# First stage of a hybrid diffusion block: modulation weights first, turning product with the row factor, projections in step, and decay rows laid out contiguously

## The chip, the cores and the metric

One core of a Trainium2 chip runs the whole program. The metric is device microseconds of one execution, lower is better. The engines are TensorE (PE, with its weight loads PEld), VectorE (DVE), ScalarE (ACT), GpSimd (POOL) and SyncE (SP), which issues nearly all DMAs. Each engine works through its own instructions in order; SP's DMAs go out in order on one queue that 16 DMA engines serve.

## The reference, cut to what matters

One layer of a diffusion backbone for 1024 tokens and 256 context tokens of width 1024. Each token row is normalised and modulated, projected by `w_in`, mixed by three branches (S5, Mamba-2, RG-LRU), merged by gates, and passed to a mixture of experts.

```python
def _rmsnorm(x, g):
    y = x32 * lax.rsqrt(jnp.mean(x32 * x32, axis=-1, keepdims=True) + EPS)
    return (y * g).astype(x.dtype)
def _modulate(x, g, shift, scale):          # shift, scale: columns of silu(c) @ w_mod + b_mod
    return _rmsnorm(x, g) * (1 + scale) + shift
proj = h @ p['w_in']                        # u_s5, z, xbc, dt_raw, x_lru, g_lru, gates
# Mamba-2, per chunk of 128 tokens, direction and head:
lmat = jnp.exp(_segsum(a))                  # exp of differences of cumulated decays, masked
y_diag = einsum(cb * lmat, xs);  y_off = einsum(cm, entering) * exp(a_cum)
```

## The kernel before, in words

All matrix products with large weights are made of two parts: the weight and the activation are split into a rounded part (`hi`, type fp32r) and a rest (`lo`), and `mm3` (L265 to L267) multiplies hi·hi, hi·lo and lo·hi.

**First stage (L154 to L254).** SP issues in this order: the eight 128x1024 row tiles of x (`xts`, half a MB each) with small parameters between them, the raw weights of two `u` projections, eight 1 MB pieces `wm` of the modulation weight, two context tiles, the `dt` weight. `x_norm` squares a row tile on ACT, gets the row factor by DVE and POOL, and scales the tile on DVE. PE turns it in 128x128 blocks by transposes (`xtb`), and ACT and DVE copy the blocks into `xh0`. When `wm` has landed, PE multiplies it with silu(c) (`pm`), and the columns `gs` and `modT` are made. `modulate` (L222 to L225) then makes `hxh` on ACT, the full value on DVE and `hxl` on DVE or POOL, for two halves of 512 tokens and, from the turned context, `hch` and `hcl`. The `dt` projection multiplies unsplit values (`pdt`, fp32) in four column groups of 32. The planner (a simulated timeline at build time) orders the instructions of each engine by priority and readiness.

**Second stage, `p1` (L290 to L657).** Tables of S5 powers (`lam`, `arai`, `pw`, `den`, `cB`), then the projections `u`, `xb`, `xl`, `gl` by `proj_chunk`, and the S5 scans by `s5_tab` and `s5_dat`.

**Third stage, `p2` (L683 to L945).** The states of Mamba-2 (`states`, tiles `xk`, `xd`, `st`), then 32 times `chunk(g, c)` (L785 to L831), with z and gate projections (`pj_z`, `pj_gt`), RG-LRU (`lps`, `lr`, `li`) and the rest of the modulation (`wm`, `pm`, L909, L912) between them. `chunk` loads a 512 KB tile `rowb`: for two directions and four heads the cumulated decays of 128 tokens, repeated on all 128 partitions. ACT makes `dec` of it (L796), eight DVE instructions subtract a column of `XL` and limit (L801), ACT takes the exponential (L802), POOL adds the directions (L803), DVE multiplies with `pcb` (L804), POOL scales `dec` (L805), and PE multiplies (`yps`, L814 and L815). The three buffers of `rowb` come round in turn. The row source `rowsd` is written once, [4 groups, 2 directions, 4 heads, 1024 tokens].

Of the kernel before, what the change touches and what calls it, by code (L numbers as in the profile page):

```python
# [18 lines left out]
P = 128  # L19
# [11 lines left out]
NEP = 4  # L31
NHI = 4
# [7 lines left out]
HXP = (1, 4, 7)  # L40
HXC = (0, 2, 4, 6)
# [4 lines left out]
LAG = 2  # L46
MEN = {mybir.EngineType.DVE, mybir.EngineType.Pool, mybir.EngineType.Activation, mybir.EngineType.PE}
# [17 lines left out]
def backbone(ctx: ExitStack, tc: tile.TileContext, I, out, dbg=None, stop=None):  # L65
# [19 lines left out]
    def bank(name):  # L85
        return bankh[0](name)
# [22 lines left out]
    dtb = cp.tile([P, 1], F32, name="dtb")  # L109
# [32 lines left out]
    pre = {}

    def x_load(i):
        Y.dma_start(xts[i], dap(I["x"] if i < 8 else I["ctx"], (i % 8) * P * D, [[D, P], [1, D]]))

    def x_norm(i):
        xt = xts[i]
        jk = p0x.tile([P, D], mybir.dt.bfloat16, tag="jk", name=f"jk{i}", bufs=1)
        A.activation(jk, xt, AF.Square, accum_out=ss[:, i:i + 1])  # L150
        v = p0x.tile([P, 2], F32, tag="v", name=f"v{i}", bufs=10)
        V.tensor_scalar(xt, xt, rstd_of(ss[:, i:i + 1], v), None, op0=ALU.mult)

    with tc.high_priority(offset=20000):  # L154
        with tc.tile_pool(name="p0", bufs=1, reuse_waits="tile") as p0:
            wms = [p0.tile([P, 2048], F32, name=f"wm{j}") for j in range(KC)]
# [10 lines left out]
            for i in range(8):  # L167
                x_load(i)
# [3 lines left out]
            for q in range(2):  # L172
                pre[f"u{q}"] = load_w(I["w_in"], 7200, OFF_U + q * P, P, KC, f"u{q}")
            for j in range(KC):
                Y.dma_start(wms[j], dap(I["w_mod"], j * 6 * D, [[KC * 6 * D, P], [1, 2048]]))
            for i in range(8, 10):
                x_load(i)
            Y.dma_start(wdt, dap(I["w_in"], OFF_DT, [[7200, P], [P * 7200, KC], [1, 32]]))
            for j in range(4):
                Y.dma_start(dtb[32 * j:32 * j + 32, :], dap(I["m2_dt_bias"], 0, [[1, 32], [1, 1]]))  # L180
            A.activation(scc, craw, AF.Silu)
            pm = bank("pm")
            V.memset(pm, 0.0)
            for i in range(8):
                x_norm(i)
                for h in range(2):
                    tb = bank(f"xtb{i}_{h}")
                    for q in range(4):
                        k = 4 * h + q
                        T.transpose(tb[:, q * P:(q + 1) * P], xts[i][:, k * P:(k + 1) * P], ident)  # L190
                    dst = xh0[:, 4 * h:4 * h + 4, i * P:(i + 1) * P]
                    (V.tensor_copy if h else A.copy)(dst, tb.rearrange("p (q c) -> p q c", q=4))
# [8 lines left out]
            mrow = p0x.tile([98, 512], F32, name="mrow")  # L201
# [20 lines left out]
        def modulate(k, e, src, t, hh, ll, E):  # L222
            A.activation(hh, src, AF.Identity, bias=modT[:, k, e:e + 1], scale=gs[:, k, e:e + 1])
            V.tensor_scalar(t, src, gs[:, k, e:e + 1], modT[:, k, e:e + 1], op0=ALU.mult, op1=ALU.add)
            E.tensor_sub(ll, t, hh.bitcast(F32))  # L225

        for h in range(2):
            sl = slice(h * 512, (h + 1) * 512)
            for k in range(KC):
                x_ = xh0[:, k, sl]  # L230
                modulate(k, 0, x_, x_, hxh[k][:, sl], hxl[k][:, sl], G if k in HXP else V)
        for i in range(8, 10):
            x_norm(i)
        for k in range(KC):
            tb = bank(f"xtc{k}")
            for i in range(2):
                T.transpose(tb[:, i * P:(i + 1) * P], xts[8 + i][:, k * P:(k + 1) * P], ident)
            modulate(k, 1, tb[:, 0:256], xc0[:, k, :], hch[k], hcl[k], G if k in HXC else V)

        pdt = psp.tile([P, 512], F32, tag="pm", name="pdt", bufs=1)  # L240
        for o, ng, n, src in ((0, 4, 256, xh0), (256, 2, P, xc0)):
            for k in range(KC):
                for j in range(ng):
                    T.matmul(pdt[32 * j:32 * j + 32, o:o + n], wdt[:, k, :], src[:, k, j * n:(j + 1) * n], start=(k == 0), stop=(k == KC - 1))
        dtT = xts[0]
        A.activation(dtT[:, 0:256], pdt[:, 0:256], AF.Identity, bias=dtb)
        A.activation(dtT[0:64, 256:384], pdt[0:64, 256:384], AF.Identity, bias=dtb[0:64])
        pd = bank("pd")
        dv = dt.rearrange("p (c e) -> p c e", c=10)
        for h in range(2):  # L250
            T.transpose(pd[:, h * P:(h + 1) * P], dtT[:, h * P:(h + 1) * P], ident)
            V.tensor_copy(dv[:, h:8:2], pd[:, h * P:(h + 1) * P].rearrange("p (j e) -> p j e", j=4))
        T.transpose(pd[:, 256:320], dtT[0:64, 256:384], ident[:64, :64])
        V.tensor_copy(dv[:, 8:10], pd[:, 256:320].rearrange("p (j e) -> p j e", j=2))  # L254
# [34 lines left out]
    with tc.tile_pool(name="p1", bufs=1, reuse_waits="tile") as p1:  # L289
        NT = 19  # L290
        lam = p1.tile([P, 2, 32], F32, name="lam")
        pl = bank("pl")
        for e, nm in enumerate(("s5_lam_re", "s5_lam_im")):
            ln = p1.tile([32, 2, 64], F32, tag="ln", name=f"ln{e}", bufs=2)
            Y.dma_start(ln, dap(I[nm], 0, [[64, 32], [2048, 2], [1, 64]]))
            T.transpose(pl[:, e * 32:(e + 1) * 32], ln.rearrange("g d p -> g (d p)"), ident[:32, :32])
        V.tensor_copy(lam, pl[:, 0:64].rearrange("p (e g) -> p e g", e=2))
        step = p1.tile([P, 32], F32, name="step")
        for d in range(2):
            Y.dma_start(step[64 * d:64 * d + 64, :], dap(I["s5_log_step"], 32 * d, [[0, 64], [1, 32]]))  # L300
# [355 lines left out]
    if dbg is not None:  # L656
        emit("s5", s5_dram)  # L657
# [903 lines left out]
```

## Time and profile before

| what | value |
|---|---|
| median of 3 runs | 2121.89 us (2120.39 to 2122.43) |
| the profiled execution | 2120.92 us, span 2119.1 us |
| PE busy in the span | 1919.3 us, 91% |
| DVE, ACT, POOL busy | 1525.2, 1020.3, 510.4 us |
| first stage ends on PE with the last `pj_u` product | 96.1 us |
| chunks of the third stage | 680 to 1040 us |
| mean granted clock of TensorE | 0.956 |

The span is the profiled part of the profiled execution; 1.8 us lie around it. A busy PE is one with a product in flight, not one at its peak, and its speed follows the granted clock: 1.00 is 2.4 GHz, 0.50 is 1.2 GHz.

### The profile page before, as it was taken

The page shows a single profiled execution, that of the slowest core. Times are in us where ns is not written, and L with a number is a line of the kernel's source. Part 1 is how long each engine was busy: PE and PEld are TensorE (multiplying, and loading weights), DVE is VectorE, ACT ScalarE, POOL GpSimd, SP SyncE. Part 2 cuts the span into 40 slices and gives each one's busy share as a digit, 9 for nine tenths or more (in the row PEclk, how much of TensorE's full clock was granted, in tenths as well). Part 3 has the DMA queues.
Part 4 walks back from the last instruction along what each step waited for, and adds up shares of the span by engine and source line. Part 5 has one row for each costly group of instructions (what it writes and reads, how often), then busy time and mean ns, then how long its engine had stood idle before and what let it go on. Part 6 is the DMA issues. An engine that isn't in the chain of part 4 may idle for free.

```text
span 2119.1 us, 27213 instructions
## 1 busy us (share of the span) xinstructions
PE 1919.3 (91%) x9630; PEld 1516.2 (72%) x9630; DVE 1525.2 (72%) x2232; ACT 1020.3 (48%) x1313; POOL 510.4 (24%) x489
## 2 busy tenths in 40 slices
PE   5989999988889988879999999898299999999997
PEld 2678888877657666456577888687188888888885
DVE  4787788783454777667434655628899999999998
ACT  4434434432213665446332212222188888888785
POOL 1353333330142344233100000234501111100122
PEclk9999999999999999989999999999599999999999
DMA  8234334422586676777666554554599999999983
GB/s 313 54 81 114 101 95 117 122 90 90 180 261 192 186 212 175 242 180 210 208 174 188 180 160 153 186 200 149 196 339 381 400 389 404 387 389 393 391 312 137
DMA packets 301554, 462.67 MB, mean 218 GB/s; under 512 B 39945, under 2 KB 200121, under 8 KB 300393
## 3 DMA queue, kind: packets, MB, share of 16 engines
q1 hardware_dynamic: 297096, 445.19, 62.2%
q0 software_dynamic: 4320, 15.73, 2.9%
q8 instruction: 76, 1.25, 0.2%
q14 instruction: 62, 0.50, 0.1%
HBM read 384.44 MB, written 78.51 MB: 218 GB/s over the span
## 4 chain that ended last, share of the span: by engine, by line
PE 55%; DMA 9%; DVE 7%; issue 2%; ACT 1%; SPq 1%; POOL 1%; DVEq 0%; ACTq 0%; POOLq 0%
PE h_w L1443 6%; PE h_w L1445 6%; PE h_w L1444 6%; PE wo L1268 3%; DMA rowb<-rowsd 3%; PE py_w L1445 3%; PE py_w L1443 3%; PE py_w L1444 3%; PE pj_gt L267 2%; PE pj_gt L265 2%; PE pj_gt L266 2%; DMA wm<-in_w_mod_dram 2%; PE bom L266 1%; PE bom L265 1%; PE st L752 1%
## 5 line engine op out<-in xcount | busy, mean ns | idle before, releaser
L1338 DVE TENSOR_TENSOR el_w<-er_w,eh_w 128x1024 fp32r<-128x1024 f32 x384 | 460.7, 1220 | 25.0 <-ACT eh_w L1337 11.1
L1337 ACT CAST eh_w<-er_w 128x1024 fp32r<-128x1024 f32 x384 | 403.7, 1052 | 135.4 <-PE h_w L1444 58.9
L1443 PE MATMUL h_w<-eh_w,thi_x 128*128 128x512 f32 x512 | 202.9, 396 | 0.0
L1445 PE MATMUL h_w<-el_w,thi_x 128*128 128x512 f32 x512 | 200.2, 391 | 0.0
L1444 PE MATMUL h_w<-eh_w,tlo_x 128*128 128x512 f32 x512 | 199.8, 390 | 0.0
L801 DVE SCALAR_TENSOR_TENSOR rowb<-rowb,XL,lim 128x128 f32<-128x128 f32 x256 | 116.1, 518 | 72.1 <-ACT dec L796 72.1
L265 PE MATMUL pj_gt<-hxh,whi_gt 128*128 128x512 f32 x384 | 155.9, 406 | 11.9 <-ACT gz L779 11.9
L267 PE MATMUL pj_gt<-hxh,wlo_gt 128*128 128x512 f32 x384 | 155.3, 404 | 0.0
L266 PE MATMUL pj_gt<-hxl,whi_gt 128*128 128x512 f32 x384 | 155.1, 404 | 0.0
L1445 PEld LDWEIGHTS h_w<-el_w,thi_x 128*128 128x128 f32 x512 | 96.2, 188 | 20.4
L1444 PEld LDWEIGHTS h_w<-eh_w,tlo_x 128*128 128x128 f32 x512 | 96.5, 188 | 19.6 <-DVE tlo_x L1362 0.4
L1443 PEld LDWEIGHTS h_w<-eh_w,thi_x 128*128 128x128 f32 x512 | 96.5, 188 | 19.2 <-ACT thi_x L1361 0.2
L265 PEld LDWEIGHTS pj_gt<-hxh,whi_gt 128*128 128x128 f32 x384 | 74.4, 194 | 38.0 <-ACT gz L779 16.1
L1346 POOL DMA_INDIRECT xs<-h2d,idx x16 | 23.3, 1459 | 309.5 <-PE tb_x L1354 294.4
L1443 PE MATMUL py_w<-eh_w,thi_h 128*128 128x512 f32 x240 | 96.3, 401 | 0.0
L1445 PE MATMUL py_w<-el_w,thi_h 128*128 128x512 f32 x240 | 94.0, 392 | 0.0
L1444 PE MATMUL py_w<-eh_w,tlo_h 128*128 128x512 f32 x240 | 93.5, 390 | 0.0
L267 PEld LDWEIGHTS pj_gt<-hxh,wlo_gt 128*128 128x128 f32 x384 | 74.4, 194 | 25.4 <-issue 9.6
L266 PEld LDWEIGHTS pj_gt<-hxl,whi_gt 128*128 128x128 f32 x384 | 74.4, 194 | 20.5 <-issue 4.9
L796 ACT ACTIVATE dec<-rowb 64x512 f32<-64x512 f32 x64 | 40.2, 629 | 82.7 <-DMA rowb<-rowsd 72.7
L267 PE MATMUL pj_xb<-hxh,wlo_xb 128*128 128x512 f32 x192 | 76.8, 400 | 0.5 <-DVE wlo_xb L128 0.5
L265 PE MATMUL pj_xb<-hxh,whi_xb 128*128 128x512 f32 x192 | 76.7, 399 | 0.0
(653 smaller groups left out, 4894.7 us busy)
## 6 DMA issues: line engine op xcount, KB each, us to landing
er_w<-in_moe_w_dram SPq DMA_DIRECT2D x384, 512.0 KB
wm<-in_w_mod_dram SPq DMA_DIRECT2D x32, 512.0 KB
rowb<-rowsd SPq DMA_DIRECT2D x32, 512.0 KB
raw_gt<-in_w_in_dram SPq DMA_DIRECT2D x24, 512.0 KB
gtd<-gz SPq DMA_DIRECT2D x48, 256.0 KB
xk<-xed SPq DMA_DIRECT2D x18, 512.0 KB
wm<-in_w_mod_dram SPq DMA_DIRECT2D x8, 1024.0 KB
xe<-xed SPq DMA_DIRECT2D x32, 256.0 KB
```

The source lines that it names most:

```text
L265: T.matmul(ps, wh(k), xh(k), start=(first and k == 0), stop=False)
L266: T.matmul(ps, wh(k), xl(k), start=False, stop=False)
L267: T.matmul(ps, wl(k), xh(k), start=False, stop=(last and k == nk - 1))
L796: A.activation(dec[64 * d:64 * d + 64], rowb[64 * d:64 * d + 64, d], AF.Exp)
L801: V.scalar_tensor_tensor(rowb[:, d, h], rowb[:, d, h], XL[:, c, d, 4 * g + h:4 * g + h + 1], lim[:, d], op0=ALU.subtract, op1=ALU.min)
L1268: T.matmul(st4[i]["ps"][n], ms[i][a][:, k], wo[k][b][:, sl], start=(k == 0 and q == 0), stop=(k == KC - 1 and q == 2))
L1337: A.copy(a, raw)
L1338: V.tensor_sub(b, raw, a.bitcast(F32))
L1346: G.indirect_dma_start(out=xsb[e], out_offset=None, in_=h2d[:, :], in_offset=bass.IndirectOffsetOnAxis(ap=idx[:, e:e + 1], axis=0))
L1443: T.matmul(ps[n], xa[:, j, :], a[:, sl], start=(j == 0), stop=False)
L1444: T.matmul(ps[n], xb[:, j, :], a[:, sl], start=False, stop=False)
L1445: T.matmul(ps[n], xa[:, j, :], b[:, sl], start=False, stop=(j == KC - 1))
```

## The change

The first stage gets its order for DVE, ACT and PE as it is written. SP first loads the small S5 inputs and c, then all of `wm`, then x0 to x3, the raw weights of `u`, x4 to x7; the context tiles are loaded into the slots of x2 and x3 once these have been turned. The S5 tables are made in this stage ahead of `pm`. x isn't scaled any more: a diagonal tile `dg` holds the row factors, and a full fp32 product of x with `dg` turns and scales at once. `modulate` reads that product from PSUM, uses no POOL, and the `u` products follow two steps behind it. The `dt` projection moves into `p1`, behind the `u` stores, and takes the split activations with a 64-column split weight. In `p2`, `rowsd` is laid out so that what one chunk needs lies in 4 KB without a gap; two whole-tile DVE instructions replace the eight, and the add goes from POOL to DVE.

```diff
+    def x_dg(i):
+        dgs[i] = p0x.tile([P, P], F32, tag="dg", name=f"dg{i}", bufs=8)
+        V.tensor_scalar(dgs[i], ident, rss0[i], None, op0=ALU.mult)
...
+    with tc.high_priority(offset=20000), tc.manual_schedule(engines=MEN3):
...
+            for j in range(KC):
+                Y.dma_start(wms[j], dap(I["w_mod"], j * 6 * D, [[KC * 6 * D, P], [1, 2048]]))
...
+            for i in range(8):
                 x_load(i)
+                for q in range(2 if i == 3 else 0):
+                    uraw.append(wp.tile([P, KC, P], F32, tag="raw", name=f"raw_u{q}", bufs=3))
+                    Y.dma_start(uraw[q], dap(I["w_in"], OFF_U + q * P, [[7200, P], [P * 7200, KC], [1, P]]))
...
+        def modulate(k, e, src, t, hh, ll):
+            sc, bi = gs[:, k, e:e + 1], modT[:, k, e:e + 1]
+            A.activation(hh, src, AF.Identity, bias=bi, scale=sc)
+            if k in HXA:
+                A.activation(t, src, AF.Identity, bias=bi, scale=sc)
+            else:
+                V.tensor_scalar(t, src, sc, bi, op0=ALU.mult, op1=ALU.add)
+            V.tensor_sub(ll, t, hh.bitcast(F32))
+        def turned(tiles, k):
+            tb = bank(f"xt{tiles[0]}k{k}")
+            for q, i in enumerate(tiles):
+                T.matmul(tb[:, q * P:(q + 1) * P], xts[i][:, k * P:(k + 1) * P], dgs[i], start=True, stop=True)
+            return tb[:, 0:len(tiles) * P]
...
+        for i in range(4):
+            x_sq(i)
+            if i > 0:
+                x_dg(i - 1)
+        u_cast(0)
+        x_dg(3)
+        for hf in range(3):
...
+                tb = turned(tiles, k)
...
+                if (hf, k) >= (0, 2):
+                    ready(*divmod(8 * hf + k - 2, 8))
+                    drain(1 if hf == 1 else 2)
...
+        for c in range(10):
+            T.matmul(pd[:, 32 * c:32 * c + 32], dtT[c // 4][0:64, (c % 4) * P:(c % 4 + 1) * P], twice, start=True, stop=True)
...
-            Y.dma_start(dap(rowsd, d * 4 * S, [[8 * S, 4], [S, 4], [1, S]]), rw[16 * d:16 * d + 16])
+            for g in range(4):
+                Y.dma_start(dap(rowsd, g * 8 * S + d * 512, [[P, 4], [8 * P, 8], [1, P]]), rw[16 * d + 4 * g:16 * d + 4 * g + 4].rearrange("h (c q) -> h c q", c=8))
...
-            Y.dma_start(rowb.rearrange("p d h q -> p (d h) q"), dap(rowsd, g * 8 * S + q0, [[0, P], [S, 8], [1, P]]))
+            Y.dma_start(rowb.rearrange("p d h q -> p (d h q)"), dap(rowsd, (8 * g + c) * 8 * P, [[0, P], [1, 8 * P]]))
...
-            for d in range(2):
-                for h in range(4):
-                    V.scalar_tensor_tensor(rowb[:, d, h], rowb[:, d, h], XL[:, c, d, 4 * g + h:4 * g + h + 1], lim[:, d], op0=ALU.subtract, op1=ALU.min)
+            sh = [P, 2, 4, P]
+            V.tensor_sub(rowb, rowb, XL[:, c, :, 4 * g:4 * g + 4][:, :, :, None].to_broadcast(sh))
+            V.tensor_tensor(rowb, rowb, lim[:, :, None, :].to_broadcast(sh), op=ALU.min)
             A.activation(rowb, rowb, AF.Exp)
-            G.tensor_add(rowb[:, 0], rowb[:, 0], rowb[:, 1])
+            V.tensor_add(rowb[:, 0], rowb[:, 0], rowb[:, 1])
```

## Rows read from the trace of the kernel before

**Rows 1.** Busy time by stage: stretch, length, busy us per engine, clock, DMA share, GB/s.
```profile
0.00:49.20 49.20, 25.36 (x144) 13.01 (x145) 19.30 (x47) 22.01 (x37) 6.13 (x16) 0.91 0.94 333
49.20:96.10 46.90, 43.02 (x258) 30.43 (x257) 34.40 (x67) 25.19 (x40) 15.55 (x32) 0.91 0.18 24
96.10:140.00 43.90, 35.83 (x198) 29.27 (x197) 41.52 (x53) 13.46 (x18) 32.99 (x25) 0.92 0.42 104
560.00:600.00 40.00, 30.57 (x132) 20.22 (x129) 16.42 (x30) 7.15 (x10) 17.84 (x10) 0.87 0.73 223
680.00:1040.00 360.00, 305.79 (x1589) 220.09 (x1589) 251.12 (x367) 201.48 (x256) 126.30 (x98) 0.92 0.71 199
```

**Rows 2.** Timeline of PE, first stage: start, us, what.
```profile
21.48 1.06 PE L190 MATMUL xtb<-ident,xt 128*128 128x128 f32 x8 [0.51 <-DVE v L117]
32.46 1.04 PE L200 MATMUL pm<-wm,scc 128*2 128x512 f32 x8 [1.45 <-DMA wm<-in_w_mod_dram]
51.47 0.39 PE L265 MATMUL pj_u<-hxh,whi_u 128*128 128x512 f32 x1
51.70 0.39 PE L266 MATMUL pj_u<-hxl,whi_u 128*128 128x512 f32 x1
94.64 0.28 PE L265 MATMUL pj_u<-hch,whi_u 128*128 128x256 f32 x1
94.76 0.28 PE L266 MATMUL pj_u<-hcl,whi_u 128*128 128x256 f32 x1
96.08 0.40 PE L265 MATMUL pj_xb<-hxh,whi_xb 128*128 128x512 f32 x1
```

**Rows 3.** Timeline of DVE, first stage.
```profile
27.19 0.69 DVE L192 COPY xh<-xtb 128x512 f32<-128x512 f32 x1 [1.15 <-PE xtb L190]
47.30 0.17 DVE L211 TENSOR_TENSOR gs<-gs,pcols 128x16 f32<-128x16 f32 x1
48.94 0.69 DVE L225 TENSOR_TENSOR hxl<-xh,hxh 128x512 fp32r<-128x512 f32 x1
```

**Rows 4.** Costliest groups on the page: busy us, mean ns, idle before, releaser.
```profile
L1338 DVE TENSOR_TENSOR el_w<-er_w,eh_w 128x1024 fp32r<-128x1024 f32 x384 | 460.7, 1220 | 25.0 <-ACT eh_w L1337 11.1
L1337 ACT CAST eh_w<-er_w 128x1024 fp32r<-128x1024 f32 x384 | 403.7, 1052 | 135.4 <-PE h_w L1444 58.9
L801 DVE SCALAR_TENSOR_TENSOR rowb<-rowb,XL,lim 128x128 f32<-128x128 f32 x256 | 116.1, 518 | 72.1 <-ACT dec L796 72.1
```

**Rows 5.** The chain that ended last: start, us, what.
```profile
574.86 12.84 DMA xk<-xed
...
690.90 8.95 DMA rowb<-rowsd
...
713.38 0.43 PE yps L815 x4
```

**Rows 6.** PE's waits, 680 to 1040 us: us in total, times, longest.
```profile
PE pm L912 <- DMA wm<-in_w_mod_dram: 15.7, 4, 5.9
PE yps L814 <- DVE rowb L804: 14.8, 5, 3.5
PE pj_gt L265 <- ACT gz L779: 9.5, 5, 4.8
PE lps L878 <- ACT lr L879: 6.9, 2, 5.7
```

**Rows 7.** PE's waits, 560 to 600 us.
```profile
PE st L752 <- POOL xd L750: 9.4, 1, 9.4
```

**Rows 8.** Busy time in two short stretches, columns as in rows 1.
```profile
692.00:697.00 5.00, 5.00 (x24) 4.00 (x24) 4.22 (x8) 1.28 (x3) 1.31 (x1) 1.00 0.28 69
1374.00:1377.00 3.00, 3.00 (x15) 2.42 (x13) 2.28 (x3) 0.00 (x0) 0.00 (x0) 1.00 0.96 321
```

**Rows 9.** SP's timeline around 1374 us.
```profile
1373.32 0.38 SPq L1191 DMA_DIRECT2D bc_m<-modd  x1
```

**Rows 10.** Tile bc_m: duration ns min/median/max, first and last start.
```profile
L1182 DVE TENSOR_TENSOR r_wo<-r_wo,bc_m x4: 1212/2305/3394, 1095.4 to 1370.5; 128x1024 f32<-128x1024 f32 x4
```

More of the change, by code (lines that the diff above doesn't have):

```diff
@@ new lines, in backbone @@
+            for e in range(2):
+                T.transpose(pl[:, e * 32:(e + 1) * 32], lns[e].rearrange("g d p -> g (d p)"), ident[:32, :32])
+            V.tensor_copy(lam, pl[:, 0:64].rearrange("p (e g) -> p e g", e=2))
+            A.activation(scc, craw, AF.Silu)
+            A.activation(step, step, AF.Exp)
+            arai = p1k.tile([P, 2, 32], F32, name="arai")
+            V.tensor_mul(arai, lam, step[:, None, :].to_broadcast([P, 2, 32]))
+            a8 = p1k.tile([P, 2, 32], F32, name="a8")
@@ L182, in backbone @@
+            V.tensor_mul(cden[:, 1], den[:, 2], den[:, 0])
             pm = bank("pm")
             V.memset(pm, 0.0)
[L184 to L192, printed above, removed]
@@ L232, in backbone @@
[L232 to L244, printed above, removed]
@@ L245, in backbone @@
[L245 to L253, printed above, removed]
@@ new lines, in turned, with u_cast @@
+        def turned(tiles, k):
[3 more added lines that the diff above has]
+            return tb[:, 0:len(tiles) * P]
+        def u_cast(q):
+            hi, lo = (wp.tile([P, KC, P], F32R, tag=t, name=f"{t}_u{q}", bufs=2) for t in ("whi", "wlo"))
+            A.copy(hi, uraw[q])
+            V.tensor_sub(lo, uraw[q], hi.bitcast(F32))
+            uw.append((hi, lo))
@@ new lines, in backbone, with u_step @@
+        ups, upend = {}, ([], [])
+        def u_step(q, c, k):
+            if k == 0:
+                if c < 2:
+                    ups[q, c] = (bank if c == 1 else pbank)(f"pj_u{q}_{c}")
+                elif q == 0:
+                    uc = psp.tile([P, 512], F32, tag="pm", name="pj_uc", bufs=1)
+                    ups.update({(p, 2): uc[:, p * SC:(p + 1) * SC] for p in range(2)})
+            n = SC if c == 2 else 512
+            x, y = (hch[k], hcl[k]) if c == 2 else (t[k][:, c * 512:(c + 1) * 512] for t in (hxh, hxl))
+            w = [t[:, k, :] for t in uw[q]]
+            for o, (a, b) in enumerate(((w[0], x), (w[0], y), (w[1], x))):
+                T.matmul(ups[q, c][:, :n], a, b, start=(k == 0 and o == 0), stop=(k == KC - 1 and o == 2))
@@ L255, in backbone @@
+        ready(2, 6)
+        ready(2, 7)
+        drain(99)
     p0x.release()
@@ L329, in backbone @@
+        with tc.high_priority(offset=20000), tc.manual_schedule(engines=MEN3):
+            for c in range(3):
+                for q, u in enumerate(u0):
+                    if c < 2:
+                        A.copy(u[:, :, 32 + c:160:2], ups[q, c].rearrange("p (t w) -> p t w", w=64))
+                    else:
+                        A.copy(u[:, :, 0:32], ups[q, 2].rearrange("p (c t) -> p t c", t=8))
         pidx = p1.tile([64, 4], F32, name="pidx")
@@ L415, in backbone, with u_store @@
         yd = [dr.tile([P, 4, P], F32, name=f"yd{c}") for c in range(8)]
+        def u_store(cts, us):
+            for c, u in zip(cts, us):
+                for g in range(8):
+                    Y.dma_start(dap(ud[2 * c + g // 4], (g % 4) * 160 + 7 * 16 * 640, [[640, 16], [-16 * 640, 8], [1, 160]]), u[16 * g:16 * g + 16])
         def u_proj(*cts):
-            us = [p1.tile([P, 8, 160], F32, tag="ac", name=f"ush{c}", bufs=2) for c in cts]
+            us = [utile(c) for c in cts]
             def ev_of(u):
@@ L678, in backbone @@
     m2_dram = [dr.tile([P, 2, S], F32, name=f"m2_dram{g}") for g in range(4)]
-    rowsd = dr.tile([4, 2, 4, S], F32, name="rowsd")
+    rowsd = dr.tile([4, 8, 2, 4, P], F32, name="rowsd")
     rbd = dr.tile([1, S], F32, name="rbd")
```

256 lines of the change are left out of this document (141 added, 115 removed).

## The prediction

> **What bounds the kernel now.** I read the profile in this order: busy time by stage, the timelines of PE and DVE in the first stage, the chain that ended last, PE's waits by stage, and then short stretches of the DMA share. PE is the engine to watch. In the first 49.2 us it has little to do, because DMA is full (share 0.94, 333 GB/s) with x and the modulation weights [rows 1]. From 49.2 us to the first `xb` product at 96.08 us [rows 2] PE is busy 43.0 of 46.9 us, DMA almost idle. From 96.1 to 140 us DVE is full (41.5 of 43.9 us) and PE loses 8.1 us [rows 1]. The chain can't be followed back through the first two stages, so there PE's busy time stands in for it.
>
> In the third stage PE is idle for 360 − 305.8 = 54.2 us while the chunks run, and its mean clock is 0.92: at half speed for part of it, which costs (1 − 0.92) × 305.8 = 24.5 us more [rows 1]. The gate products are filler there and still go on behind the chunks, so whatever PE gains in the stage ends the stage earlier. The waits behind the 54.2 us [rows 6] look mixed: `wm` (15.7), `rowb` from DVE (14.8), ACT's `gz` (9.5) and `lr` (6.9). But ACT is in order, and `dec` stands in it ahead of the others, waiting for the `rowb` load; the chain shows such a load at 8.95 us [rows 5]. In 692 to 697 us, with that load in flight, the 16 DMA engines are 0.28 busy and move 69 GB/s [rows 8]. At that rate 524 KB takes 7.6 us, most of the 8.95. So the load is slow by itself, while three quarters of the engines stand idle, and everything issued behind it on SP waits. This is what I take for the real limit of the stage.
>
> **First stage.** The first turning product now needs `wm` (8.39 MB), x0 to x3 (2.10 MB) and, because `u_cast(0)` stands ahead of `x_dg(3)` in DVE's fixed order, the first raw `u` weight (0.52 MB): 11.0 MB at 333 GB/s [rows 1] is 33 us. For the small loads now ahead I add 2 us (0 to 5, an estimate from the difference between 333 GB/s and a full DMA share). Then come a cast of 1.05 us and a subtraction of 1.22 us [rows 4] and the diagonal, under 1 us: PE starts at about 38 us; before, `gs` was ready at 47.5 us [rows 3].
>
> From there PE has 80 turning products. A full fp32 product of 128 columns goes by in 0.43 / 2 = 0.215 us, since four records are two products [rows 5]; those have 64 columns of weights, so with wider weights it may take up to twice that. I take 0.215, nearest in operation: 17.2 us (34 at the upper end). The transposes that they replace took 1.06 / 8 = 0.133 us [rows 2], but lay under the loads. The Trainium skill, "TensorE: Matmul & The Clock Gate", section Terms, speaks against this edit: it calls the transpose mode four times faster for fp32. By that the 80 products would take 42.6 us and the sum would be 25 us worse; the row above shows a ratio of 1.6, and no row here has the exact shape.
>
> The `u` products are unchanged: 2 × 2 × 8 × 3 = 96 of 512 columns at 0.23 us and 48 of 256 at 0.12 us [rows 2], 27.6 us. Together 44.8 us, plus 4 us for a mean clock of 0.91 as in the stage before [rows 1], 1 us for the ends: `u` is done at 88 us. DVE is no limit if PE is: 14 instructions of about 0.6 us per half [rows 3] and the second weight's 1.22 us are under 11 us, against 15 us of PE (32 turning and 36 `u` products) in the first half. POOL's share of the subtractions is gone, which DVE takes over within this.
>
> The `dt` projection leaves this stretch, where it cost PE time between 49 and 75 us, and comes back behind `u`: 32 products of 512 columns at 0.23, 16 of 256 at 0.12, ten short ones at about 0.1, 10.3 us. So `xb` has PE to itself from 98 us instead of 96.1: 2 us lost. The gain is elsewhere: the S5 tables now lie under the loads, where DVE has 30 us to spare, as has ACT [rows 1]. Of the stretch to 140 us, 8.1 us of waiting and (1 − 0.92) × 35.8 = 2.9 us of clock can come back; I take 10, because DVE was full there. Net −8 us, bounds −20 (start at 33 us, all returned) and +18 (turning products at twice the price, no relief).
>
> The later context load waits until x2 and x3 are turned, some 15 us after the start, and is needed another 12 us later; behind it on SP stand only weights for `xb`, wanted at 88 us. I cost it at nothing; uncovered, it would be one load, about 3 us.
>
> **Decay rows: the load.** The new load has 4 KB per partition without a gap. The nearest row is `bc_m`, with the same form (one 4 KB row repeated on 128 partitions): issued at 1373.32 us [rows 9], and in 1374 to 1377 us the engines are 0.96 busy at 321 GB/s [rows 8], with weights ahead of it in flight. So I expect 1.6 us of transfer instead of 7.6, a landing of 3 to 4 us. The 32 loads then leave the queue 32 × 6 = 192 us of narrow use. What returns is at most 54.2 + 24.5 = 78.7 us, at least about 10. I take 60%, 47 us: all waits listed but `wm` hang on ACT or DVE behind `dec`, `wm` on the same queue, but DMA stays 0.7 busy, so bursts will still make some loads late. What is late next is `wm` and the transfers of the gates.
>
> **Decay rows: the arithmetic.** Eight instructions per chunk cost 116.1 / 32 = 3.63 us of DVE [rows 4]. Two 128x1024 instructions at 1.22 [rows 4] and one add at 0.69 [rows 3] are 3.13 us: 16 us less in 32 chunks on an engine with 109 us to spare, and one crossing to POOL less. It counts only as part of the 47. The upper price is 3.39 us, a 128x1024 DVE instruction beside POOL work [rows 10].
>
> **Decay rows: the states.** In 560 to 600 us PE waits 9.4 us for `xd` [rows 7], which waits for an `xk` load that takes 12.84 us behind three `rowb` loads [rows 5]; the clock of 0.87 costs 0.13 × 30.6 = 4 us [rows 1]. That is 13.4 us to have back. Against it, `rowsd` is written by eight DMAs instead of two; at 0.4 to 0.8 us an issue (0.38 for one of the plainest, [rows 9]) that is 2.5 to 5 us ahead of the first `rowb`. Net −9, bounds −13 and 0.
>
> **Sum.** −8 − 9 − 47 = −64 us. On the profiled execution's span, 2119.1 − 64 = 2055, plus 1.8 us around it: 2057 us. The profiled execution is 1 us below the median of the runs shown, which I leave in the range. About 0.2% (4 us) is what a measurement here can tell from no change.
>
> **Rivals.** *Another wait takes the place.* DMA is 0.71 busy among the chunks [rows 1]; in a shorter stage it is near 0.8, and `wm` and gate transfers keep PE waiting. Then 20 us come back there, 5 at the states, 4 in front: 2121 − 29 = 2092. For it: 15.7 us of waits for `wm` [rows 6]. Against: the share holds stretches of 0.28 only because of the load in question.
>
> *All of it comes back*: −79 − 13 − 11 gives 2018. For it: every wait listed touches the queue.
>
> *The load stays narrow.* All partitions still read the same bytes, and if that is what holds it at 69 GB/s, only the front (−8) and the shorter DVE work (−5) are left, with 2 us for the extra stores: 2110. Against it stands `bc_m`. The Trainium skill, "DMA: Bandwidth & Descriptors", section "Why a DMA increments its semaphore by 16 and not by 1", lets the slowest dimension decide how many engines a transfer gets; that is 128 partitions in both forms, 16 engines, so by it the new form would gain nothing here, though the 0.28 of the trace does not fit it either.
>
> *DVE becomes the bound, slower.* If the two whole-tile instructions run at 3.39 us beside POOL's `dec` products and RG-LRU, DVE has 251.1 − 116.1 + 32 × (2 × 3.39 + 0.69) = 374 us of work in a stage of 360 [rows 1]: +14, with −8 in front 2127. It decides from (360 − 135 − 22) / 64 = 3.17 us on; the old instructions beside the same POOL work ran at 0.518 us on the mean [rows 4], so I doubt it.
>
> *The steps keep PE at 1.2 GHz.* If waits between the steps hold the clock down, the 44.8 us become 90, 41 more than costed: −64 + 41 gives 2098. In the stretch before, the clock was 0.91 with a similar mix [rows 1].
>
> **Chances and range.** The forecast 0.50 (its own range 2035 to 2080), another wait 0.18, all of it 0.14, narrow load 0.07, DVE 0.06, slow steps 0.05. Of the narrow load's 0.07, 0.03 is within 0.2%, where the front's 8 us fail too. So faster 0.91, same 0.03, slower 0.06. The range takes in the first three cases and the slow steps: 2013 to 2099.
>
> **What would show it.** The first turning product near 38 us, the last `u` product near 88, and no table instructions on DVE behind it. `xk` landing in under 5 us at the states. Among the chunks: no stretch of DMA share 0.3 with a `rowb` in flight, ACT's waits for `rowb` under 20 us, PE idle under 30 us, the clock over 0.95, the chunks done in about 310 us. I am wrong if a `rowb` still takes 9 us, if the whole-tile instructions take over 2 us, or if the planner's new order opens waits in `p1` that no row here shows.

## The result and the profile after

The changed kernel takes 2052.61 us (median of 4 runs, 2048.95 to 2057.03), the kernel before on the same chip 2122.14 us: a ratio of 0.9675, 95% interval 0.9655 to 0.9695. That is 69.5 us less; the forecast was 64 less, 2057 us. The profiled execution's span went from 2119.1 to 2051.4 us, the mean granted clock from 0.956 to 0.971.

To see where it came back, I followed one product of PE at each stage's end in both traces and counted how much earlier it stands (its start, in us) after the change:

| last product of | before | after | earlier by | gained in this stage | forecast |
|---|---|---|---|---|---|
| `xb` (second stage) | 372.6 | 367.6 | 5.0 | 5.0 | 8 |
| `gl` (end of the second stage) | 523.5 | 518.2 | 5.3 | 0.3 | 0 |
| `st` (states) | 664.6 | 647.1 | 17.5 | 12.2 | 9 |
| `yps` (chunks) | 1036.9 | 976.3 | 60.6 | 43.1 | 47, with the gates |
| `pj_gt` (gates behind the chunks) | 1129.6 | 1064.6 | 65.0 | 4.4 | |
| `h_w` from `thi_x` (experts) | 2067.2 | 1999.5 | 67.7 | 2.7 | 0 |

The busy time by stage in the changed kernel, with the columns of [rows 1]:

```profile
96.10:140.00 43.90, 43.20 (x287) 34.20 (x286) 33.58 (x41) 12.27 (x18) 34.58 (x26) 0.97 0.27 67
560.00:600.00 40.00, 40.00 (x169) 25.08 (x168) 24.93 (x23) 8.69 (x12) 21.04 (x9) 1.00 0.88 265
680.00:1000.00 320.00, 300.74 (x1604) 218.49 (x1603) 255.51 (x218) 192.11 (x247) 109.19 (x67) 0.98 0.72 226
```

From 96.1 to 140 us DVE is no longer full (33.6 us, 41.5 before [rows 1]), and PE is: 43.2 of 43.9 us. In 560 to 600 us PE has no wait left; the 9.4 us for `xd` [rows 7] are gone and the clock is 1.00. Among the chunks PE is idle 320 − 300.7 = 19.3 us where it was 54.2, at 0.98 of the clock where it was 0.92 (the chunks now run from 660 to 977 us, and there it is idle for 317 − 297.7 = 19.3 us too); the DMA engines move 226 GB/s at the share of before, 0.72. What PE still waits for there, in 640 to 1000 us (total, times, longest), against [rows 6]:

```profile
PE yps L896 <- DVE rowb L886: 8.5, 5, 3.4
PE yps L896 <- issue: 4.0, 2, 2.0
PE pm L994 <- DMA wm<-in_w_mod_dram: 3.9, 2, 3.4
```

ACT's wait for the load of `rowb` in that stretch is 13.3 us in 7 waits, 63.2 before (two groups). One of the loads, to set beside the one of [rows 8]: SP issues it at 734.97, and ACT's `dec` can start at 739.92. The lines are the window 735 to 740 us, SP's timeline and ACT's timeline:

```profile
735.00:740.00 5.00, 4.94 (x32) 3.33 (x30) 5.00 (x6) 0.61 (x2) 1.32 (x1) 1.00 0.95 320
```
```profile
734.97 0.38 SPq L875 DMA_DIRECT2D rowb<-rowsd  x1
```
```profile
739.92 1.27 ACT L878 ACTIVATE dec<-rowb 64x512 f32<-64x512 f32 x2 [4.39 <-DMA rowb<-rowsd]
```

With a `rowb` and other loads in flight the engines are now 0.95 busy at 320 GB/s, where they were 0.28 at 69 [rows 8]. What is left of this wait is queueing behind a full DMA, not a narrow load. The new DVE instructions on the tile `rowb` have the costed duration at the median (1.226, 1.224 and 0.682 us), but not in the sum. Their lines from 560 to 980 us, with busy us and mean ns:

```profile
L883 DVE TENSOR_TENSOR rowb<-rowb,lim 128x1024 f32<-128x1024 f32 x32 | 52.9, 1654 | 0.4
L882 DVE TENSOR_TENSOR rowb<-rowb,XL 128x1024 f32<-128x1024 f32 x32 | 51.0, 1595 | 40.5 <-ACT dec L878 40.5
L885 DVE TENSOR_TENSOR rowb<-rowb 128x512 f32<-128x512 f32 x32 | 26.1, 816 | 7.1 <-ACT rowb L884 7.0
```

Together they take 130 us of DVE, 4.06 us a chunk, where the eight old ones took 116.1 [rows 4]. Why, experiment 4 shows.

PE's timeline in the first stage (start, us, what, idle before and releaser):

```profile
35.50 0.49 PE L309 MATMUL xt0k<-dg,xt 128*128 128x128 f32 x2 [1.92 <-DVE dg L166]
...
39.71 4.21 PE L309 MATMUL xt0k<-dg,xt 128*128 128x128 f32 x18 [1.21 <-DVE dg L166]
...
46.13 1.05 PE L309 MATMUL xt0k<-dg,xt 128*128 128x128 f32 x8
48.41 1.05 PE L309 MATMUL xt0k<-dg,xt 128*128 128x128 f32 x8
...
89.46 0.28 PE L332 MATMUL pj_uc<-hch,wlo_u 128*128 128x256 f32 x1
89.58 0.38 PE L461 MATMUL cb<-ident,cld 128*128 128x128 f32 x2
94.05 0.48 PE L461 MATMUL cb<-ident,cld 128*128 128x128 f32 x1 [4.08 <-DMA cld<-in_s_c_re_dram]
94.89 0.69 PE L721 MATMUL pdt<-hxh,wd 128*64 128x512 f32 x1 [0.37 <-DVE wd L715]
...
108.71 0.48 PE L387 MATMUL pj_xb<-hxh,whi_xb 128*128 128x512 f32 x1
```

The first turning product stands at 35.5 us, and they run on without a stop once the diagonal of x3 is there (39.71; 38 was forecast). From 46.13 to 48.41 us PE does one step, four turning products (eight records) and six `u` products at 0.23 us: (2.28 − 6 × 0.23) / 4 = 0.22 us for a turning product. The last product of `u` is at 89.46 us (88 was forecast). Then PE turns the first two of S5's eight `c` tiles (`cld`), waits 4.08 us for the third, the `dt` projection follows with its first products 0.43 us apart, 0.23 later (the granted clock is 0.59 in 95 to 100 us, so mostly the lower level, 1.2 GHz), and `xb` starts at 108.71 instead of the forecast 98.

### The profile page after: what moved, and what is told of

Its sections match the earlier page's. It is cut to its first block, busy times and chain, and to the rows that moved or that the text cites. A ratio compares the mean times of both kernels' runs of the same rounds, so it can differ in the third digit from the quotient of the medians.

```text
span 2051.4 us, 27085 instructions
## 1 busy us (share of the span) xinstructions
PE 1901.4 (93%) x9679; PEld 1517.1 (74%) x9679; DVE 1527.0 (74%) x2070; ACT 1018.1 (50%) x1311; POOL 482.1 (24%) x447
## 4 chain that ended last, share of the span: by engine, by line
PE 59%; DVE 7%; DMA 3%; ACT 2%; issue 2%; SPq 1%; POOL 1%; DVEq 0%; ACTq 0%
PE h_w L1525 6%; PE h_w L1527 6%; PE h_w L1526 6%; PE wo L1350 3%; PE py_w L1527 3%; PE py_w L1525 3%; PE py_w L1526 3%; PE pj_gt L387 2%; PE pj_gt L389 2%; PE pj_gt L388 2%; PE st L834 2%; PE bom L387 1%; PE bom L388 1%; PE bom L389 1%; PE pj_z L387 1%
## 5 line engine op out<-in xcount | busy, mean ns | idle before, releaser
L1526 PEld LDWEIGHTS h_w<-eh_w,tlo_x 128*128 128x128 f32 x512 | 96.5, 188 | 19.5 <-DVE tlo_x L1444 0.4
L1525 PEld LDWEIGHTS h_w<-eh_w,thi_x 128*128 128x128 f32 x512 | 96.5, 188 | 19.1 <-ACT thi_x L1443 0.2
L388 PEld LDWEIGHTS pj_gt<-hxl,whi_gt 128*128 128x128 f32 x384 | 72.6, 189 | 19.3 <-issue 4.1
L887 POOL TENSOR_TENSOR dec<-dec,bc 128x512 f32<-128x512 f32 x32 | 65.2, 2038 | 88.7 <-ACT dec L878 77.3
L882 DVE TENSOR_TENSOR rowb<-rowb,XL 128x1024 f32<-128x1024 f32 x32 | 51.0, 1595 | 40.5 <-ACT dec L878 40.5
```

The source lines that it names most:

```text
L388: T.matmul(ps, wh(k), xl(k), start=False, stop=False)
L882: V.tensor_sub(rowb, rowb, XL[:, c, :, 4 * g:4 * g + 4][:, :, :, None].to_broadcast(sh))
L887: G.tensor_mul(dec, dec, Cd[:, None, :].to_broadcast([P, 4, P]))
L1525: T.matmul(ps[n], xa[:, j, :], a[:, sl], start=(j == 0), stop=False)
L1526: T.matmul(ps[n], xb[:, j, :], a[:, sl], start=False, stop=False)
```

## Experiments

Times of the kernel before beside these runs: 2120.53, 2119.5 and 2120.62 us in the three groups of runs. The first four runs divide the change.

**1. The decay rows alone.** The kernel before with the diffs of experiments 3 and 4 together.

> The kernel before with all of the decay-row edits and none of the first stage. Theory (the decay rows carry the gain, the first stage about 5 to 8 us): some 60 us faster, about 2062 us. Rival (the first stage carries more than its own 5 us, because an earlier start also loosens the later stages): under 45 us faster, above 2077 us.

Measured: 2060.49 us, ratio 0.9718 (0.9699 to 0.9738), 60.0 us less. In its trace the states gain 11.8 us (last `st` at 652.9 with the first one unmoved), the chunks, from first to last `yps`, take 319.4 us instead of 360.6.

**2. The front alone.** The changed kernel with the diffs of experiments 3 and 4 undone.

> The changed kernel with the old layout, load and arithmetic of the decay rows: the first stage alone. Theory: 5 to 10 us faster than before, about 2114 us, with the last product of the second stage's gl projection 5 us earlier than before. Rival (the first stage carries more): over 20 us faster, below 2102 us.

Measured: 2114.82 us, ratio 0.9977 (0.9967 to 0.9987), 5.7 us less; the last `gl` product stands 6.5 us earlier (517.0). 5.7 and 60.0 make 65.7, against 69.5 measured for both; the two halves hardly depend on one another.

**3. The load alone.**

```diff
-    rowsd = dr.tile([4, 2, 4, S], F32, name="rowsd")
+    rowsd = dr.tile([4, 8, 2, 4, P], F32, name="rowsd")
-            Y.dma_start(dap(rowsd, d * 4 * S, [[8 * S, 4], [S, 4], [1, S]]), rw[16 * d:16 * d + 16])
+            for g in range(4):
+                Y.dma_start(dap(rowsd, g * 8 * S + d * 512, [[P, 4], [8 * P, 8], [1, P]]), rw[16 * d + 4 * g:16 * d + 4 * g + 4].rearrange("h (c q) -> h c q", c=8))
-            Y.dma_start(rowb.rearrange("p d h q -> p (d h) q"), dap(rowsd, g * 8 * S + q0, [[0, P], [S, 8], [1, P]]))
+            Y.dma_start(rowb.rearrange("p d h q -> p (d h q)"), dap(rowsd, (8 * g + c) * 8 * P, [[0, P], [1, 8 * P]]))
```

> The kernel before with only the new layout of rowsd and the load of 4 KB per partition; the eight DVE instructions and POOL's add stay. Theory (the narrow load was the limit): at least 40 of the 60 us, about 2075 us, and ACT's waits for the rowb load fall from 63 to under 25 us. Rival (the shorter chain on DVE and the missing crossing to POOL were the limit): under 15 us faster, above 2107 us.

Measured: 2068.17 us, ratio 0.9755 (0.9738 to 0.9772), 52.4 us less. The load alone brings most of it.

**4. The arithmetic alone.**

```diff
-            for d in range(2):
-                for h in range(4):
-                    V.scalar_tensor_tensor(rowb[:, d, h], rowb[:, d, h], XL[:, c, d, 4 * g + h:4 * g + h + 1], lim[:, d], op0=ALU.subtract, op1=ALU.min)
+            sh = [P, 2, 4, P]
+            V.tensor_sub(rowb, rowb, XL[:, c, :, 4 * g:4 * g + 4][:, :, :, None].to_broadcast(sh))
+            V.tensor_tensor(rowb, rowb, lim[:, :, None, :].to_broadcast(sh), op=ALU.min)
-            G.tensor_add(rowb[:, 0], rowb[:, 0], rowb[:, 1])
+            V.tensor_add(rowb[:, 0], rowb[:, 0], rowb[:, 1])
```

> The kernel before with only the two whole-tile DVE instructions and the add on DVE; layout and load stay as they were. Theory (narrow load): within 10 us of before, 2112 to 2122 us, since DVE still waits for the same load. Rival (arithmetic): 40 us faster, about 2080 us. A third view, DVE beside POOL becomes slow: slower than before, the whole-tile instructions over 2 us on the mean.

Measured: 2124.72 us, ratio 1.0026 (1.0013 to 1.0038), 4.2 us *more*. The third view had the sign right; the mean of the whole-tile instructions is 1.34 us for the subtraction and 1.88 for the minimum. The minimum, alone on the tile here (duration in ns, min/median/max), then an instruction of POOL, and two of the minima, one beside it and one with POOL idle:

```profile
L801 DVE TENSOR_TENSOR rowb<-rowb,lim x32: 1195/2194/3331, 580.3 to 1036.9; 128x1024 f32<-128x1024 f32 x32
```
```profile
679.92 2.34 POOL L805 TENSOR_TENSOR dec<-dec,bc 128x512 f32<-128x512 f32 x1 [9.34 <-ACT dec L796]
```
```profile
681.13 2.20 DVE L801 TENSOR_TENSOR rowb<-rowb,lim 128x1024 f32<-128x1024 f32 x1
706.95 1.21 DVE L801 TENSOR_TENSOR rowb<-rowb,lim 128x1024 f32<-128x1024 f32 x1
```

The one at 681.13 starts while POOL's product runs (until 682.26) and ends 1.07 us behind it; at 706.95 POOL is idle, and the instruction takes 1.21 us. Nearly all follow this: of the 64 whole-tile instructions (subtraction and minimum) 26 started beside a running POOL instruction here, and 25 of them ended 1.08 us after it; the other 38 took 1.20 to 1.23 us. In the changed kernel it is 25 of 28, and 36 at 1.19 to 1.23 us. No slow one started beside an idle POOL, so a slow instruction is one that waited for POOL's to end. For the minimum that is 20 of 32 times here and 15 of 32 in the changed kernel, which puts the medians (2.19 and 1.22 us) on different sides of a gap; the means are 1.88 and 1.65.

Added to the faster load, the same edit takes 2068.17 − 2060.49 = 7.7 us off. So its sign depends on the load. It isn't DVE's time that is saved: the three new instructions take 130 us in each of the kernels that have them, the eight old ones 116.1 us on the old load and 121.8 on the new. POOL loses its adds (42.5 and 47.7 us) and the crossing to it; that this makes the 7.7 us is not shown.

**5 to 7. What made the load narrow.** The old load reads eight pieces of 512 bytes, 4096 bytes apart, for each of 128 partitions. The packet records of the trace before hold only 512-byte packets in 692 to 697 us, 676 of them: 27 ns each at the median, 4.4 in flight on the mean and never more than 9. The 512-byte packets of the raw `u` weights, which the planner had put ahead of x, take 27 ns too in 3 to 5 us, with 18 in flight. A packet is not slow, then; too few are in flight. The packets of the two stretches:

```profile
DMA packets 676, 0.35 MB, mean 69 GB/s; under 512 B 0, under 2 KB 676, under 8 KB 676
```
```profile
DMA packets 1333, 0.67 MB, mean 337 GB/s; under 512 B 16, under 2 KB 1333, under 8 KB 1333
```

Three kernels keep eight pieces of 512 bytes and the old arithmetic, and change the distance (the second also writes its rows with eight DMAs, as the new layout does): rows padded to 4224 bytes, the new layout with 640 bytes from piece to piece, and rows padded to 4608 bytes.

```diff
-    rowsd = dr.tile([4, 2, 4, S], F32, name="rowsd")
+    PT = S + 32
+    rowsd = dr.tile([4, 8, PT], F32, name="rowsd")
...
+            Y.dma_start(rowb.rearrange("p d h q -> p (d h) q"), dap(rowsd, g * 8 * PT + q0, [[0, P], [PT, 8], [1, P]]))
```

The third has S + 128 in place of S + 32; the second has these lines:

```diff
+    PT = 160
+    rowsd = dr.tile([4, 8, 8, PT], F32, name="rowsd")
...
+                Y.dma_start(dap(rowsd, g * 64 * PT + d * 4 * PT, [[PT, 4], [8 * PT, 8], [1, P]]), rw[16 * d + 4 * g:16 * d + 4 * g + 4].rearrange("h (c q) -> h c q", c=8))
...
+            Y.dma_start(rowb.rearrange("p d h q -> p (d h) q"), dap(rowsd, (8 * g + c) * 8 * PT, [[0, P], [PT, 8], [1, P]]))
```

> The kernel before, rowsd rows padded from 4096 to 4224 bytes: rowb is still loaded as eight pieces of 512 bytes per partition, no longer 4096 bytes apart. Theory (the distance of 4096 bytes between the pieces, the same for all, holds the load down): as with the whole 4 KB rows, about 2068 us. Rival (small pieces that all partitions read from the same place are slow, wherever they lie): about 2120 us, the load still near 70 GB/s.

> The kernel before with the new layout of rowsd but every piece of 512 bytes followed by a gap of 128 bytes, so that eight separate pieces per partition remain, all within 5 KB. Distance theory: about 2068 us. Small-pieces rival: about 2120 us. If this one is fast and the one with 4224 bytes slow, it is the spread over 32 KB that counts.

> The kernel before with one edit: the rows of rowsd stand 4608 bytes apart instead of 4096, so the eight 512-byte pieces of a chunk step by 4096 + 512. With 4224 bytes the time was 2082, with 640 bytes 2065, with 4096 bytes 2120 us. Theory: pieces that are a multiple of 4096 bytes apart are served by the same place in memory, and a shift by a whole piece per row frees them all: 2063 to 2070 us, ACT's wait for rowb near 16 us. Rival: it is the spread of the pieces over 32 KB that costs, and 4224 had only part of its loss from the distance: 2078 to 2086 us, ACT's wait near 44 us.

| pieces apart | 4096 B | 4224 B | 4608 B | 640 B | no gap |
|---|---|---|---|---|---|
| us | 2120 | 2082.35 | 2068.89 | 2065.48 | 2068.17 |
| ratio, interval | 1 | 0.9827, 0.9796 to 0.9859 | 0.9757, 0.9739 to 0.9774 | 0.9748, 0.9718 to 0.9778 | 0.9755, 0.9738 to 0.9772 |

The wait that ended with a landing of `rowb`, all engines together (us, times), in the order of the table, the kernel before first:

```profile
  DMA rowb<-rowsd: 72.7, 14
```
```profile
  DMA rowb<-rowsd: 43.8, 9
```
```profile
  DMA rowb<-rowsd: 23.8, 7
```
```profile
  DMA rowb<-rowsd: 16.2, 4
```
```profile
  DMA rowb<-rowsd: 15.3, 3
```

With 640 bytes the load has as many packets and the same repeated bytes as before and is as good as the one without a gap. So neither the size of the pieces nor that 128 partitions read the same bytes made it narrow; the distance of 4096 bytes did. With 4224 bytes 2068 us were expected and 2082 measured. The rows with 4608 bytes are spread over more memory than those with 4224 and are better, so it isn't the spread. What in the memory does it, and why 4224 bytes help only in part, no run shows.

**8. Is the `dt` projection paid in full?** The changed kernel with one product of 16 in each of the three stretches of `dt`; the other 15 are left out.

```diff
-            for k in range(KC):
-                for q, x in enumerate((xh, xl)):
-                    T.matmul(pt[0:64, 0:n], wd2[:, k, :], x[k][:, o:o + n], start=(k == 0 and q == 0), stop=(k == KC - 1 and q == 1))
+            T.matmul(pt[0:64, 0:n], wd2[:, 0, :], xh[0][:, o:o + n], start=True, stop=True)
```

> The changed kernel with the moved dt projection cut to one product of sixteen for each stretch of tokens (dt then holds an eighth of its sum, rounded parts alone). Theory (PE bounds the second stage, so the 10 us of dt products are paid in full behind the u products): about 10 us faster than the changed kernel, 2042 us. Rival (they lie in idle time of PE, which waits there for DVE anyway): under 3 us.

Measured: 2051.0 us, ratio 0.9677 (0.9654 to 0.9700); the rival came out. `xb` starts 12.2 us earlier, at 96.5, and its last product stands at 365.7 instead of 367.6. The work left out is replaced by idle time: busy time in two stretches, the changed kernel and then this one:

```profile
110.00:140.00 30.00, 29.52 (x217) 24.63 (x216) 23.29 (x29) 7.59 (x10) 24.44 (x19) 1.00 0.11 29
140.00:200.00 60.00, 58.78 (x383) 50.14 (x381) 43.69 (x65) 25.07 (x35) 20.33 (x24) 1.00 0.47 126
```
```profile
110.00:140.00 30.00, 26.78 (x214) 22.33 (x214) 25.08 (x32) 8.72 (x11) 21.81 (x17) 1.00 0.25 60
140.00:200.00 60.00, 58.00 (x377) 49.85 (x377) 44.37 (x65) 24.79 (x35) 19.81 (x21) 0.97 0.42 113
```

PE looks full in the changed kernel, and still it isn't what sets the end of `xb`: without `dt` it gets through the same work hardly sooner, with 2.7 us more idle in the first stretch, 0.8 in the second, and 0.03 × 58 = 1.7 us of clock.

**9. Do the tables under the loads make the front's gain?** The changed kernel with the arithmetic of the S5 tables (`lam`, `arai`, `pw`, `den`) moved back behind `u`; their loads stay early. Their scratch tiles come from slots of the second stage then.

```diff
-            lam = p1k.tile([P, 2, 32], F32, name="lam")
...
-            V.tensor_mul(cden[:, 1], den[:, 2], den[:, 0])
             pm = bank("pm")
...
+        lam = p1k.tile([P, 2, 32], F32, name="lam")
...
+        V.tensor_mul(cden[:, 1], den[:, 2], den[:, 0])
         pidx = p1.tile([64, 4], F32, name="pidx")
```

> The changed kernel with the arithmetic of the S5 tables (DVE, ACT and POOL instructions, and the two small transposes) put back behind the first stage, where it was before; the loads of its inputs stay early. Theory (my prediction's step): what the front gained is the relief of DVE behind the u products, about 10 us, and without it DVE is full again from 90 to 140 us and PE waits there: 2060 to 2064 us. Rival: the 10 us are swallowed by the second stage in either place, as the dt projection was, and the time stays at 2051 to 2055; the front's 5.5 us then came from the earlier u products.

Measured: 2059.47 us, ratio 0.9712 (0.9697 to 0.9726), 6.9 us more than the changed kernel. `u` ends 2.3 us earlier (87.1) and `xb` starts 6.2 us earlier (102.5), but the last `xb` is at 372.9, where it was before the change. Where it is lost, in this kernel and then in the changed one:

```profile
96.10:140.00 43.90, 41.19 (x219) 34.62 (x217) 35.45 (x45) 10.23 (x15) 34.00 (x24) 0.80 0.18 44
...
115.00:120.00 5.00, 3.62 (x16) 3.36 (x16) 4.82 (x6) 1.90 (x4) 3.95 (x4) 0.67 0.01 2
120.00:125.00 5.00, 4.19 (x21) 3.67 (x20) 4.90 (x4) 0.00 (x0) 4.84 (x4) 0.50 0.00 0
```
```profile
115.00:120.00 5.00, 5.00 (x23) 4.14 (x23) 5.00 (x8) 0.59 (x1) 4.92 (x4) 1.00 0.00 0
120.00:125.00 5.00, 5.00 (x57) 4.22 (x56) 3.57 (x6) 1.95 (x3) 4.76 (x4) 1.00 0.00 0
```

PE has 219 products and transposes in the stretch instead of 287, and a clock of 0.80 instead of 0.97: behind `u` it had stood 3.7 us waiting for `wd`, and from 115 to 125 us it was busy 7.8 of 10 us, at 0.67 and then 0.50 of the clock, where the changed kernel runs through at 1.00. So the tables do matter: without their move the time is that of the decay rows alone (2060.49 us, experiment 1). What of the 7 us is DVE's time and what the clock that PE's pauses cost isn't separated.

**10 to 12. Can the front give more?** Three versions of the changed kernel. One clears `pm` ahead of the tables and makes the diagonal of x3 ahead of the first cast; in it no DMA moves. The other two have these edits and give the eight tiles of `c` other memory, so that their loads don't wait for two slots in turn (4.08 us of PE above): in one buffer, and then in two others with the load of the `dt` weight ahead of the stores of `u`.

```diff
+            pm = bank("pm")            # ahead of the tables
+            V.memset(pm, 0.0)
...
+        x_dg(3)
         u_cast(0)
-        x_dg(3)
```

The `c` tiles and the `dt` weight of the last one:

```diff
+                cl = p1.tile([P, 4, P], F32, tag="M", name=f"cld{e}", bufs=S5B["M"])
-                    ct_ = p1.tile([P, 2, 64], F32, tag="ln", name=f"cld{e}{b}", bufs=2)
+                    ct_ = cl[:, b].rearrange("p (d q) -> p d q", d=2)
...
-        u_store((0, 1), u0)
...
         Y.dma_start(wdt, dap(I["w_in"], OFF_DT, [[7200, P], [P * 7200, KC], [1, 32]]))
         Y.dma_start(dtb[0:32, :], dap(I["m2_dt_bias"], 0, [[1, 32], [1, 1]]))
+        u_store((0, 1), u0)
```

> The changed kernel with two edits of order in the first stage: pm is cleared ahead of the S5 tables instead of behind them, and the diagonal of x3 is made ahead of the first cast of a u weight. No DMA moves. In the changed kernel the first product into pm waited 1.97 us for the clearing, and the first turning product lay at 35.50 us. Theory: the front of PE was late by what stood ahead of it in DVE's order, and in this stage nothing takes its place, so the u products end 2 to 4 us earlier (85.5 to 87.5 instead of 89.5) and most of it reaches the end: 2049 to 2051 us against 2052.6. Rival: as with the dt projection, the full second stage swallows it: the u products end earlier, the last xb product stays at 367.5 us within 1 us, and the time is 2052 to 2053.

> The changed kernel with three edits of order: the clearing of pm ahead of the S5 tables on DVE, the diagonal of x3 ahead of the first weight split, and the eight S5 c tiles loaded into one buffer instead of two slots in turn. Theory: the first turning product 1 to 2 us earlier, the wait of 4 us for the c tiles and the slow clock behind it gone, together 4 to 7 us faster than the changed kernel, about 2047 us. Rival (the time is given back at the later waits of the second stage): within 2 us of it.

> The two order edits of e_order, the eight c tiles in the two M buffers, so that their loads wait for no slot, and the dt weight's load put ahead of the 16 stores of u in SP's order. In the kernel with the c tiles in one buffer (2067.0 us) the dt weight came to be issued at 97.35 us, behind these stores. Theory: that place in SP's queue was what cost the 14 us, so with the load ahead of the stores PE meets the dt projection without a wait: 2047 to 2051 us, and no PE wait above 2 us for wd or pta between 80 and 110 us. Rival: the cost was the c tiles' own buffer and the new order that the planner made of the second stage, and the time stays near 2060 to 2067 us.

Measured: the first 2051.15 us, ratio 0.9670 (0.9656 to 0.9683); `u` ends 2.5 us earlier (87.0), the last `xb` 1.3 us earlier, and the time can't be told from that of the changed kernel. The other two are slower than it, though `u` ends earlier still: 2067.03 us (0.9754, 0.9734 to 0.9774) and 2063.3 us (0.9733, 0.9720 to 0.9747). No version beats the changed kernel by more than the measurement can tell.

SP's timeline in the changed kernel, and in the last of the three, shows what the free tiles did:

```profile
56.09 0.82 SPq L156 DMA_DIRECT2D xt<-in_ctx_dram  x2
...
64.84 2.15 SPq L460 DMA_DIRECT2D cld<-in_s_c_re_dram  x2
67.04 0.47 SPq L710 DMA_DIRECT2D wdt<-in_w_in_dram  x1
88.14 0.37 SPq L124 DMA_DIRECT2D raw_u<-in_w_in_dram  x1
...
91.92 0.39 SPq L460 DMA_DIRECT2D cld<-in_s_c_re_dram  x1
```
```profile
61.88 2.15 SPq L461 DMA_DIRECT2D cld<-in_s_c_re_dram  x3
85.21 0.37 SPq L124 DMA_DIRECT2D raw_u<-in_w_in_dram  x1
85.62 0.58 SPq L461 DMA_DIRECT2D cld<-in_s_c_re_dram  x1
...
90.10 0.47 SPq L710 DMA_DIRECT2D wdt<-in_w_in_dram  x1
```

A raw weight of `u` has no slot until DVE has split a weight of `xb` (SP stands on that for 21 us), at 85 us; everything behind it on SP waits. In the changed kernel the `dt` weight stands ahead of it, issued at 67.04 us. The planner, with the slots of `c` gone, put it behind: 90.10 us here, 97.35 in the version before it, where it stood behind the 16 stores as well. With the load ahead of these stores, and the `c` tiles in the two buffers, the time is 3.7 us less; the expectation that the stores were all of it fell. Nor did the wait for `c` go: PE has 5.4 us of it here, 4.1 in the changed kernel, since the last five of these loads stand behind the raw weight now. PE also waits 6.7 us for `wd` and 3.6 for `dtT`, starts `xb` at 125.3 us and is 12 us late at its end. That the late weight causes all of this was not tested alone.

## Why the prediction was right, step by step

**Sum.** −64 forecast, −69.5 measured, inside its own range of 2035 to 2080. Its three terms were −8, −9, −47; the trace shows −5.3, −12.2 and −47.5 (43.1 in the chunks, 4.4 in the gates behind them), and 2.7 more in the experts that no step named.

**The load.** Right: narrow by itself, and a full queue once it is contiguous (0.95, 320 GB/s). 60% of what could come back was taken, 47 of 78.7; 47.5 came back. No row gives the 60%, so that it came out this near is luck. The rival by which it stays narrow, with its 16 engines before and after, fell. The Trainium skill, "DMA: Bandwidth & Descriptors", section "Why a DMA increments its semaphore by 16 and not by 1", gives both forms the same number of engines; here 69 GB/s moved with the one form in flight and 320 with the other, so that count didn't decide. My reason, a load with gaps, was too wide: a gap of 128 bytes cost nothing that can be measured, 4096 bytes from piece to piece cost some 50 us.

**Another wait in its place.** `wm` and gate transfers didn't take it over: 3.9 us of waits for `wm` where 15.7 stood [rows 6]. *All of it comes back* was too much: 19.3 us of idle time are left in the stage.

**The arithmetic.** This step failed, though the sum counted it only as part of the 47. It took 3.13 us a chunk from rows of 1.22 and 0.69, 16 us less DVE work in all; measured are 4.06 us and 14 us more, because 25 of the 64 whole-tile instructions waited for POOL (experiment 4). The row of 3.39 [rows 10], called the upper price, is such a wait too (it ended 1.08 us after a POOL instruction), and the 0.518 that the prediction set against it is the mean of old instructions of which 44 in 256 were over 0.7 us, at a median of 0.341. The worth of the edit also changes sign: +4.2 us on the old load, −7.7 on the new. The rival of a DVE bound needed 3.17 us an instruction; single ones reached 3.38, the means are 1.60 and 1.65. Still, 21 of the 64 took over 2 us, which the prediction had listed as a sign of being wrong; the sum held because it rests on the load.

**The states.** −9 forecast from 13.4 less the price of eight stores; 12.2 measured; if all of the 13.4 came back, the stores cost 1.2 us and not the 2.5 to 5 allowed. "An `xk` lands in under 5 us" did not come out: the chain of waits still shows one of 8.57 us at 533.3, but none behind a `rowb`.

**The first stage.** The turning product was right (0.215 costed, 0.22 measured), and the starting point too: 38 forecast, 39.7 measured for the full step. The Trainium skill, "TensorE: Matmul & The Clock Gate", section Terms, calls the transpose mode four times faster for fp32; here the turning product took twice the time of a transpose. The ratio of 1.6 in the prediction sets 0.215 us from start to start against 0.133, which holds the last transpose's end. On the same terms, without the last record's 0.27 us and with the clock at 1.00 in both, a transpose (one record) takes (1.06 − 0.27) / 7 = 0.113 us [rows 2] and a turning product (two records) 2 × (1.05 − 0.27) / 7 = 0.22 us. The tile lines show the records of 64 transposes and of 32 turning products, before and after (duration in ns, min/median/max):

```profile
L190 PE MATMUL xtb<-ident,xt x64: 272/314/477, 10.9 to 26.9; 128*128 128x128 f32 x64
```
```profile
L309 PE MATMUL xt0k<-dg,xt x64: 271/275/582, 35.5 to 56.0; 128*128 128x128 f32 x64
```

`u` came out 1.5 us late.

Behind `u` two steps failed, in opposite directions. The first is that nothing but `dt` stands between `u` and `xb`. The sum has no term for S5's `c` tiles, which share two slots: the third can leave only when PE has turned the first (89.58 us), stands behind stores of `u` on SP and is issued at 91.92. PE waits 4.08 us for it and then begins `dt` at half its clock; with other S5 products between, `xb` starts at 108.7 instead of 98. The later context load isn't the cause, though S5's `b` and `c` do stand behind it on SP and not only weights for `xb`, as the prediction has it: its products begin at 71.39 us without a wait, and in experiment 10 it leaves 2.5 us earlier (53.55) and the wait for `c` is still 4.0 us. The second step is that what delays PE's start there is paid in full: the sum had +2 for the start and −10 for the relief of DVE. The trace has +12.6 for the start, and from the first `xb` product of 512 columns to the last 364.6 − 108.7 = 255.9 us where it was 369.6 − 96.1 = 273.5, so −17.6. Leaving `dt` out (experiment 8) moved the start by 12 us and the end by 2. Start and relief are not two terms that add. That other engines set the pace of the stage, and that with the tables under the loads (experiment 9) these were ahead, fits both runs; which engine it is no run shows. Their net, −5 instead of −8, was near by luck.

## What to carry to other kernels

When a load moves few bytes at a low DMA share, read the packets: if they take their usual time and only few are in flight, try the distance between the pieces: here 32 to 128 floats of padding alone brought 37 to 52 us. A PE that is 98% busy in a stage need not be what sets its end: take work out of it and see whether the end moves before costing work that is put in. A duration with two values is not described by its median: look at what ran beside each instance. An order that a planner makes around a slot (experiments 11 and 12) can undo a wait that was removed by hand; look at what stands ahead on the queue, not only at the wait.

## What the runs showed that was not expected

Pieces of 512 bytes, read by 128 partitions, ran at 69 GB/s when they lay 4096 bytes apart, with 4.4 packets of 27 ns in flight; the same number of pieces 640 bytes apart cost no more than 4 KB without a gap (2065.5 and 2068.2 us).

A whole-tile DVE instruction on `rowb` that started beside a running POOL instruction ended 1.08 us after it, in 25 of 28 cases in the changed kernel; beside an idle POOL it took 1.2 us. A median of 2.2 us in one kernel and 1.22 in another only says whether more or less than half of them waited.

The same code for the first two stages ended its last `xb` product anywhere from 368.2 to 372.8 us in the profiled executions of the kernel before and its variants in `p2`. A shift of 2 or 3 us in one trace is therefore no finding by itself; the front's gain rests on the timed ratio of experiment 2.
